# A transformer layer on one core: its first norm spread over ScalarE and GpSimd, and its first two tiles in written order

## The chip, the core and the metric

The kernel runs on one core of a Trainium2 chip. The core has five engines that are meant here: TensorE (PE, with its weight loads as PEld), VectorE (DVE), ScalarE (ACT), GpSimd (POOL), and SyncE (SP), which issues most DMAs. The metric is the device time of one execution in microseconds (us); a time given for a kernel is the median of several executions.

## What is computed

One layer of a diffusion transformer over 512 latent tokens (`x`) and 256 context tokens (`ctx`), model width 2048, all in float32. Cut to what matters here:

```python
sc_ = jax.nn.silu(c); scc = jax.nn.silu(c_ctx)
mod_x = (sc_ @ w_ada[l] + b_ada[l])[:, None, :]
mod_c = (scc @ w_ada[l] + b_ada[l])[None, None, :]
...
h  = _modulate(_rmsnorm(x, norm1_w[l]), sh1, s1)       # h * (1 + scale) + shift
hc = _modulate(_rmsnorm(xc, norm1_w[l]), sh1c, s1c)
q_da, k_da, v_da, q_mla, k_mla, v_mla = _mixer_inputs(h, tabs, *proj)
...
o_da = _sweep(lambda qb: _diff_attend(qb, k_da_all, v_da_all, lam), q_da)
o_mla = _sweep(lambda qb: _softmax_attend(qb, k_mla_all, v_mla_all, MLA_SCALE), q_mla)
x = x + g1 * (_merge_heads(o_da, o_mla, subln_w[l], lambda_init) @ w_o[l])
h2 = _modulate(_rmsnorm(x, norm2_w[l]), sh2, s2)
x = x + g2 * _conv_ffn(h2, w_up[l], conv_w[l], conv_b[l], w_down[l])
return _rmsnorm(x, final_w)
```

The normalised input needs a sum of squares over all 2048 features of each token, and a shift and a scale for each feature, which are products of `silu(c)` and `silu(c_ctx)` with columns of `w_ada`.

## The kernel before

Tokens lie along the free dimension. The 2048 features are 16 tiles (`kt`) of 128 partitions; `xs[kt]` (128x512) holds a tile of the latents, and `cs[kt // 2]` (128x512) the 256 context tokens of two tiles. A float32 product is made of three matmuls on parts (`mm3`, lines 101 to 106): each operand is split into a high part of type `F32R` (ScalarE) and the rest (VectorE, function `split`, lines 75 to 84).

**The beginning** (lines 266 to 314) stands inside `tc.manual_schedule`, so its engines take it in written order.
- SP loads the rows `c` and `c_ctx`, then all token tiles, then the first rows and columns of `w_ada`.
- ScalarE takes a Silu of both raw rows (line 282, one partition, 2048 long), TensorE spreads them over 128 partitions by a matmul with ones (line 287), and copies bring them to `cb` and `ccb` (lines 301 and 303).
- ScalarE squares each latent tile (line 293) and every second context half (line 295), VectorE squares the other halves (line 297) and adds 128x768 to one running sum `sqs` (line 299).
- TensorE sums `sqs` over the partitions by a matmul with ones (line 306). `rstd` (lines 157 to 164) makes 1/sqrt of it: Ln and Exp on ScalarE, one Newton step on VectorE. The result is `rinv`.

**Scales and shifts.** `scales(u)` makes the scale columns `a1` of two tiles by small TensorE products (`products`, line 206), a copy of `row` on ScalarE (line 208), two tiny matmuls (line 210) and a VectorE step (line 218). The shifts `modx` and `modc` of a tile come in one of two ways (`shifts`): for an even tile VectorE multiplies and reduces rows of `w_ada` (line 242, a half of 1024 at a time; one for the latents and one for the context), for an odd tile TensorE transposes the rows (line 258) and makes products. `modulation(u)` does both for two tiles and loads and splits the weights `w_g0` of these.

**The first weight products** (lines 344 to 367). For each tile VectorE makes `h` (line 358), ScalarE adds the shift and rounds to the high part (line 360), VectorE makes the low part (line 361), and TensorE adds the tile's contribution to five latent and four context accumulators (`mm3`, 27 matmuls). Outside `manual_schedule` a scheduler orders each engine's instructions.

**Later.** The other input projections follow, with the values last: their halves are split by ScalarE (`kh`) and VectorE (`kl`) and written to memory `v_d` (line 498), in the second half by GpSimd's queue. Then the first attention (`da_head`): the query, key and value parts of a head are read back (lines 543 to 558), with keys in `ks` and in the half-zero tile `klz` (cleared on GpSimd, line 534), scores are matmuls of line 510, the maximum is VectorE's (line 512), the exponential ScalarE's (line 514). `feature` makes the queries of the next head from `w_f` and calls `ahead(2)`, which issues the loads of the next weight blocks.

Of the kernel before, what the change touches and what calls it, by code (L numbers as in the profile page):

```python
# [17 lines left out]
P = 128  # L18
# [34 lines left out]
def layer_kernel(ctx: ExitStack, tc: tile.TileContext, small, rope, c_row, cc_row, x_t, ctx_t, ada, ada_k,  # L53
# [32 lines left out]

    def wblock(src, cols=1024, pool=None):
        pool, full = (pool, cols) if pool else (wp, 1024)
        raw = pool.tile([P, full], F32, tag="wr", name=nm("wr"), bufs=3 if full == 1024 else 2)
        nc.sync.dma_start(raw[:, :cols], src)  # L90
# [66 lines left out]
    def rstd(out, ssq, dim, t1, t2):  # L157

        sc.activation(out, ssq, AF.Ln, bias=epst, scale=1.0 / dim)
        sc.activation(out, out, AF.Exp, scale=-0.5)  # L160
        ve.tensor_scalar(out=t1, in0=ssq, scalar1=1.0 / dim, scalar2=EPS, op0=ALU.mult, op1=ALU.add)
# [50 lines left out]
    def scales(u, ws=None):  # L212

        ws = ws or columns(u)
# [6 lines left out]
    def columns(u):  # L221
        ws = []
        for j in range(4):
# [13 lines left out]
    def shift(kt, ws, i):  # L237

        d, vec = (modx, modc)[i][:, kt:kt + 1], (cb, ccb)[i]
        for hf, w in enumerate(ws):  # L240
            t = w if i else st.tile([P, D // 2], BF16, tag="junk", name=nm("junk"), bufs=1)
            ve.tensor_tensor_reduce(out=t, in0=w, in1=vec[:, hf * D // 2:(hf + 1) * D // 2], op0=ALU.mult,
                                    op1=ALU.add, scale=1.0, scalar=d if hf else col("b_ada", kt), accum_out=d)

    def shifts(kt):
# [4 lines left out]
        if kt % 2 == 0:  # L250
            for i in range(2):
                shift(kt, ws, i)
# [10 lines left out]

    with tc.manual_schedule(engines={mybir.EngineType.PE, mybir.EngineType.Activation, mybir.EngineType.DVE,
                                     mybir.EngineType.SP}):
# [9 lines left out]
        first_rows, first_columns = rows(0), columns(0)  # L277
# [3 lines left out]
        for wide in (cb, ccb):  # L281
            sc.activation(wide[0:1], wide[0:1], AF.Silu)
# [5 lines left out]
        exp_ln_tables()  # L288
        sqs = st.tile([P, TT], F32, tag="h", name="sqs", bufs=3)
        for kt in range(KT):  # L290
            sq = st.tile([P, TT], F32, tag="h", name=nm("sq"), bufs=3) if kt else sqs
            c = cs[kt // 2][:, (kt % 2) * C:(kt % 2 + 1) * C]
            sc.square(sq[:, :T], xs[kt])
            if kt % 2:
                sc.square(sq[:, T:], c)
            else:
                ve.tensor_tensor(sq[:, T:], c, c, op=ALU.mult)
            if kt:
                ve.tensor_tensor(sqs, sqs, sq, op=ALU.add)
            if kt in (8, 10, 12, 14):  # L300
                ve.tensor_copy(*spread.pop(0))
        while spread:
            sc.copy(*spread.pop(0))
        ssq = s_tile()
        for c0, c1 in ((0, T), (T, TT)):
            pe.matmul(ssq[:, c0:c1], ones32, sqs[:, c0:c1], start=True, stop=True)
        shift(0, first_rows, 0)
# [4 lines left out]
    g0b = [b_tile() for _ in range(4)]  # L312
    acc = g0b[3]
    g0w = []

    def modulation(u):
        if u:
            shifts(2 * u)
        scales(u, None if u else first_columns)
        g0w.append(wblock(w_g0[2 * u], 640, st))  # L320
        shifts(2 * u + 1)
        g0w.append(wblock(w_g0[2 * u + 1], 640, st))

    modulation(0)
    nc.sync.dma_start(silu_c, cb[0:1])
    nc.sync.dma_start(ropet, rope)
# [13 lines left out]
    hx, hc = [], []  # L340
    g0s = [s_tile(), s_tile()]
    lat0 = [g0s[0][:, :512], g0s[0][:, 512:], g0s[1][:, :512], g0s[1][:, 512:], g0b[0]]
    ctx0 = [g0b[1][:, :C], g0b[1][:, C:], g0b[2][:, :C], g0b[2][:, C:]]
    for kt in range(KT):
        if kt % 2 == 0 and kt < KT - 2:
            modulation(kt // 2 + 1)
        ct = cs[kt // 2][:, (kt % 2) * C:(kt % 2 + 1) * C]
        if kt % 2 == 0:
            chh, chl = c2k(F32R), c2k(F32R)
        o = (kt % 2) * C  # L350
        hx.append((a2k(F32R), a2k(F32R)))
        hc.append((chh[:, o:o + C], chl[:, o:o + C]))
        with tc.high_priority():
            h = st.tile([P, TT], F32, tag="h", name=nm("h"), bufs=3)
            for i, (x, c, m, (hh, hl)) in enumerate(((xs[kt], slice(0, T), modx, hx[kt]),
                                                     (ct, slice(T, TT), modc, hc[kt]))):
                b, t, r = m[:, kt:kt + 1], h[:, c], rinv[:, c]
                ve.scalar_tensor_tensor(out=t, in0=x, scalar=a1[:, 2 * kt + i:2 * kt + i + 1], in1=r,
                                        op0=ALU.mult, op1=ALU.mult)
                sc.activation(hh, t, AF.Identity, bias=b)  # L360
                ve.scalar_tensor_tensor(out=hl, in0=t, scalar=b, in1=hh.bitcast(F32), op0=ALU.add, op1=ALU.subtract)
        wh, wl = g0w[kt]
        for f in range(5):
            w = (wh[:, f * P:(f + 1) * P], wl[:, f * P:(f + 1) * P])
            mm3(lat0[f], w, hx[kt], kt == 0, kt == KT - 1)
            if f < 4:
                mm3(ctx0[f], w, hc[kt], kt == 0 and f % 2 == 0, kt == KT - 1, skip=True)
# [89 lines left out]
    def feature(lat, ctxo):  # L457
# [8 lines left out]
        ahead(2)  # L466
# [63 lines left out]

    klz = [da.tile([P, 2, TT], F32R, name=nm("klz")) for _ in range(2)]
    for t in klz:
        for i, r in enumerate((hi, lo)):
            gp.memset(t[r, i].bitcast(F32), 0.0)
# [4 lines left out]
    def da_queries(h):  # L539
        if h == 0:  # L540
            qs = [da.tile([P, T], F32R, tag=f"qs{i}", name=nm("qs"), bufs=2) for i in range(2)]
            for i in range(2):
                nc.sync.dma_start(qs[i].bitcast(F32), q0_d[i])
            return qs
        lat = b_tile("f", 2)
        feature(lat, None)
# [4 lines left out]
    def da_head(h, qs):  # L551
        ks = da.tile([P, 2, TT], F32R, tag="ks", name=nm("ks"), bufs=2)
        kl = klz[h % 2]
        for i, r in enumerate((lo, hi)):
            nc.sync.dma_start(ks[r].bitcast(F32), k_d[h][0].rearrange("(i p) n -> p i n", i=2))
            nc.sync.dma_start(kl[r, i].bitcast(F32), k_d[h][1][r])
# [857 lines left out]
```

## Time and profile before

| What | us |
|---|---|
| median of 3 executions | 2441.83 (2437.65 to 2445.8) |
| profiled execution, its own time | 2441.33 |
| its span in the profile | 2439.6 |
| TensorE busy | 2367.0 (97%) |
| VectorE busy | 1735.5 (71%) |
| ScalarE busy | 1117.0 (46%) |
| GpSimd busy | 220.2 (9%) |
| mean granted TensorE clock | 0.992 |

A timeline row gives the start in us from the span's start, the time it took, the engine, the line of the kernel, the operation, `out<-in` by tile names, the size, and how often it follows itself; in brackets the time for which the engine sat idle before it and what ended that. A float32 matmul of the row "x4" is two matmuls of two passes each. A row of waits reads: engine and line, what it waited for, us in total, times, longest. Matmuls overlap, so their steps are read from start to start.

### The profile page before, as it was taken

The numbers are of one execution on the slowest core, as the hardware profiler recorded it, in microseconds if no ns is written. First come the engines' busy times: TensorE is split into PE (matmuls) and PEld (weight loads), VectorE is DVE, ScalarE is ACT, GpSimd is POOL, SyncE is SP. The second block draws the span as 40 slices with busy tenths as digits, with TensorE's granted clock in tenths as the row PEclk, the third lists the DMA queues.
The fourth block names the chain that finished last, engine by engine and source line by source line (L and its number), as shares of the span: only waits on it lengthen the run. The fifth ranks groups of instructions, "written<-read, shape, count | busy, mean of one in ns | idle before, by whom it ended". The sixth has DMA issues, their size and how long they took to land.

```text
span 2439.6 us, 32889 instructions
## 1 busy us (share of the span) xinstructions
PE 2367.0 (97%) x12758; PEld 1978.4 (81%) x12758; DVE 1735.5 (71%) x2316; ACT 1117.0 (46%) x1696; POOL 220.2 (9%) x244
## 2 busy tenths in 40 slices
PE   6999999999999999999999999999999999999998
PEld 3678877777777778889888888888888888888888
DVE  6668876388868878378667676767666666666667
ACT  4432121155646542245445454545454545454545
POOL 0000000121100003100111111111111111111110
PEclk9999999999999999999999999999999999999999
DMA  8758889555411149423555555555555565556573
GB/s 300 279 211 309 327 319 330 181 166 144 127 59 44 44 161 349 146 87 113 147 130 143 134 140 137 137 139 136 141 134 143 132 143 132 141 135 140 133 188 111
DMA packets 130707, 403.32 MB, mean 165 GB/s; under 512 B 14323, under 2 KB 25075, under 8 KB 122099
## 3 DMA queue, kind: packets, MB, share of 16 engines
q1 hardware_dynamic: 104118, 350.87, 43.7%
q0 software_dynamic: 25280, 49.30, 11.6%
q8 instruction: 100, 1.64, 0.3%
q10 hardware_dynamic: 1152, 1.05, 0.1%
q14 instruction: 57, 0.47, 0.1%
HBM read 331.68 MB, written 69.48 MB: 164 GB/s over the span
## 4 chain that ended last, share of the span: by engine, by line
PE 76%; DVE 8%; issue 7%; ACT 4%; DMA 3%; POOL 2%; SPq 0%; DVEq 0%; ACTq 0%; POOLq 0%
PE y L1133 11%; PE b L105 9%; PE b L104 9%; PE b L106 9%; PE z L1133 5%; PE y L1135 5%; PE s L104 3%; PE s L105 3%; PE s L106 3%; PE z L1135 3%; PE s L510 3%; PE x L1133 2%; DMA ada<-in_ada 2%; PE b L206 1%; PE f L104 1%
## 5 line engine op out<-in xcount | busy, mean ns | idle before, releaser
L989 DVE TENSOR_TENSOR wl<-wr,wh 128x1024 fp32r<-128x1024 f32 x144 | 176.4, 1225 | 157.8 <-ACT wh L981 157.1
L981 ACT CAST wh<-wr 128x1024 fp32r<-128x1024 f32 x144 | 151.0, 1049 | 234.0 <-PE b L105 118.5
L104 PE MATMUL b<-ah,wh 128*128 128x512 f32 (+1 forms) x664 | 256.8, 387 | 0.0
L105 PE MATMUL b<-al,wh 128*128 128x512 f32 (+1 forms) x664 | 256.7, 387 | 0.0
L106 PE MATMUL b<-ah,wl 128*128 128x512 f32 (+1 forms) x664 | 255.9, 385 | 0.0
L1154 POOL DMA_DIRECT2D x_d<-xs x160 | 139.6, 1004 | 1162.6 <-ACT xs L1153 1159.3
L989 DVE TENSOR_TENSOR wl<-rb,wh 128x1024 fp32r<-128x1024 f32 x123 | 150.0, 1220 | 126.9 <-ACT wh L981 126.8
L981 ACT CAST wh<-rb 128x1024 fp32r<-128x1024 f32 x123 | 129.2, 1050 | 185.7 <-PE b L105 116.1
L989 DVE TENSOR_TENSOR wl<-ws,wh 128x1024 fp32r<-128x1024 f32 x123 | 150.1, 1220 | 90.1 <-ACT wh L981 90.1
L80 ACT CAST wh<-wr 128x1024 fp32r<-128x1024 f32 (+3 forms) x102 | 99.2, 972 | 217.0 <-PE b L106 62.1
L171 DVE CUSTOM_DVE_ANT_0 ada<-ada,cb,smt 128x2048 f32<-128x2048 f32 x64 | 152.5, 2382 | 54.6 <-DMA ada<-in_ada 54.2
L981 ACT CAST wh<-ws 128x1024 fp32r<-128x1024 f32 x123 | 128.2, 1043 | 130.3 <-DVE ws L943 44.3
L1133 PE MATMUL y<-a2k,wh 128*128 128x512 f32 x656 | 164.0, 392 | 0.0
L81 DVE TENSOR_TENSOR wl<-wr,wh 128x1024 fp32r<-128x1024 f32 (+3 forms) x102 | 116.9, 1146 | 62.1 <-ACT wh L80 61.7
L104 PE MATMUL b<-a2k,wh 128*128 128x512 f32 (+1 forms) x376 | 141.6, 377 | 5.9 <-ACT a2k L838 4.3
L106 PEld LDWEIGHTS b<-ah,wl 128*128 128x128 f32 x664 | 124.8, 188 | 25.7
L104 PEld LDWEIGHTS b<-ah,wh 128*128 128x128 f32 x664 | 125.1, 188 | 22.9
L105 PEld LDWEIGHTS b<-al,wh 128*128 128x128 f32 x664 | 125.1, 188 | 21.9
L105 PE MATMUL b<-a2k,wh 128*128 128x512 f32 (+1 forms) x376 | 140.8, 374 | 0.0
L106 PE MATMUL b<-a2k,wl 128*128 128x512 f32 (+1 forms) x376 | 140.0, 372 | 0.0
L1133 PEld LDWEIGHTS y<-a2k,wh 128*128 128x128 f32 x656 | 118.6, 189 | 21.6
L1133 PE MATMUL y<-b2k,wh 128*128 128x512 f32 x410 | 107.8, 393 | 0.0
(454 smaller groups left out, 5757.2 us busy)
## 6 DMA issues: line engine op xcount, KB each, us to landing
ada<-in_ada SPq DMA_DIRECT2D x64, 1024.0 KB, 6.4
rb<-in_w_up SPq DMA_DIRECT2D x123, 512.0 KB, 4.3
wr<-in_w_dn SPq DMA_DIRECT2D x88, 512.0 KB, 4.3
x_d<-xs POOLq DMA_DIRECT2D x160, 256.0 KB, 6.0
wr<-in_w_up SPq DMA_DIRECT2D x53, 512.0 KB, 4.2
wr<-in_w_f SPq DMA_DIRECT2D x34, 512.0 KB, 6.0
ada<-in_ada SPq DMA_DIRECT2D x32, 512.0 KB, 6.4
adak<-in_ada_k SPq DMA_DIRECT2D x32, 512.0 KB, 6.3
```

The lines of the kernel that those rows point to most:

```text
L80: sc.copy(dst_h, src)
L81: ve.tensor_tensor(dst_l, src, dst_h.bitcast(F32), op=ALU.subtract)
L104: pe.matmul(out, st[0], mv[0], start=start, stop=False, **kw)
L105: pe.matmul(out, st[0], mv[1], start=False, stop=False, **kw)
L106: pe.matmul(out, st[1], mv[0], start=False, stop=stop, **kw)
L171: ve.tensor_tensor_reduce(out=junk, in0=w, in1=vec, op0=ALU.mult, op1=ALU.add, scale=1.0, scalar=col("b_ada", j), accum_out=dst[:, j:j + 1])
L510: pe.matmul(s[:, c0:c1], a, b[:, c0:c1], start=i == 0, stop=i == len(mms) - 1)
L981: sc.copy(t, raw[:, k * n_:k * n_ + n_])
L989: ve.tensor_tensor(t, raw[:, k * n_:k * n_ + n_], hi[k].bitcast(F32), op=ALU.subtract)
L1133: pe.matmul(o, w[j][0], hs[j], start=start and j == 0, stop=False, skip_group_check=True)
L1135: pe.matmul(o[:, h0], w[j][1], hs[j][:, h0], start=False, stop=j == 7, skip_group_check=True)
L1154: gp.dma_start(x1_d[dt], x, accum_op=ALU.add)
```

## The change

- **Raw rows.** TensorE spreads the raw `c` and `c_ctx`, and ScalarE takes the Silu of the spread rows as it moves them out of PSUM (128x512 each, eight of them), between its squares.
- **Squares.** Each latent square goes to a tile of its own, so ScalarE does not wait for VectorE. GpSimd squares the context tiles (128x512, two tiles at once). VectorE keeps two running sums, one of the latents and one of the context; the last two latent squares are not added by VectorE but go to TensorE's column sums, which become five matmuls.
- **`rstd`** takes a piece of work to put between its VectorE steps: the first half of tile 0's shift.
- **Written order.** The first two tiles, with shifts of both by VectorE, `scales(0)`, `scales(1)` and the first products, now stand inside `manual_schedule`, which holds GpSimd too. Their loads are issued in written order. In tiles 0 and 1 the five latent products stand ahead of the four context ones. `modulation(1)` keeps shifts and weights of tiles 2 and 3 alone; `silu_c` and `ropet` are moved behind it.
- **First attention.** Tiles of the pool `da` are laid out in another order, `klz` is cleared by VectorE, and the loads of the weight blocks behind head 1's queries are issued after the key loads of head 0.

```diff
-    def rstd(out, ssq, dim, t1, t2):
+    def rstd(out, ssq, dim, t1, t2, beside=None):
...
         ve.tensor_scalar(out=t1, in0=ssq, scalar1=1.0 / dim, scalar2=EPS, op0=ALU.mult, op1=ALU.add)
+        if beside:
+            beside()
         ve.scalar_tensor_tensor(out=t2, in0=out, scalar=-0.5, in1=out, op0=ALU.mult, op1=ALU.mult)
...
-            sc.activation(wide[0:1], wide[0:1], AF.Silu)
...
-        for kt in range(KT):
-            sq = st.tile([P, TT], F32, tag="h", name=nm("sq"), bufs=3) if kt else sqs
-            c = cs[kt // 2][:, (kt % 2) * C:(kt % 2 + 1) * C]
-            sc.square(sq[:, :T], xs[kt])
-            if kt % 2:
-                sc.square(sq[:, T:], c)
+        for p in range(KT // 2):
+            qc = c2k()
+            gp.tensor_tensor(qc, cs[p], cs[p], op=ALU.mult)
+            if p >= 6:
+                sc.activation(*spread[p], AF.Silu)
+            qs = [square(2 * p), square(2 * p + 1)]
+            if p < 6:
+                sc.activation(*spread[p], AF.Silu)
+            if p == 0:
+                sx, sc_ = qs[0], qc
             else:
-                ve.tensor_tensor(sq[:, T:], c, c, op=ALU.mult)
-            if kt:
-                ve.tensor_tensor(sqs, sqs, sq, op=ALU.add)
+                ve.tensor_tensor(sc_, sc_, qc, op=ALU.add)
+            for q in qs[p == 0:]:
+                if p == KT // 2 - 1:
+                    sums.append(q)
+                else:
+                    ve.tensor_tensor(sx, sx, q, op=ALU.add)
...
+        for i, q in enumerate([sx] + sums):
+            pe.matmul(ssq[:, :T], ones32, q, start=i == 0, stop=i == 2)
+            if i == 1:
+                for j in range(2):
+                    pe.matmul(ssq[:, T:], ones32, sc_[:, j * C:j * C + C], start=j == 0, stop=j == 1)
...
-        rstd(rinv, ssq[:, :TT], D, nt1, nt2)
-        shift(0, first_rows, 1)
+        rstd(rinv, ssq, D, nt1, nt2, lambda: shift(0, first_rows[0], 0, 0))
+        shift(0, first_rows[0], 0, 1)
...
+        for kt in range(2):
+            homes(kt)
+            if kt:
+                for hf in range(2):
+                    shift(1, first_rows[1], 0, hf)
+                g0w.append(split_block(raw1, 640, st))
+            scaled(kt, 0)
+            scaled(kt, 1)
+            shifted(kt, 0)
+            for hf in range(2):
+                shift(kt, first_rows[kt], 1, hf)
+            shifted(kt, 1)
+            if kt:
+                scales(1, second_columns)
+            g0_products(kt)
...
-        ahead(2)
+        with tc.issue_after(behind) if behind else nullcontext():
+            ahead(2)
...
-            gp.memset(t[r, i].bitcast(F32), 0.0)
+            ve.memset(t[r, i].bitcast(F32), 0.0)
+    key_loads = []
```

Here `scaled(kt, i)` is the `h` step of the latents (`i` = 0) or the context (1), `shifted(kt, i)` the high and low parts, `shift(kt, ws, i, hf)` one half of a VectorE reduction, and `g0_products(kt)` the 27 matmuls of a tile.

How it moves instructions, at three places. First VectorE at the start, before:

```order
L297 TENSOR_TENSOR sqs<-c2k_162 128x256
L299 TENSOR_TENSOR sqs<-sqs,sq_241 128x768
L297 TENSOR_TENSOR sq_245<-c2k_168 128x256
L299 TENSOR_TENSOR sqs<-sqs,sq_245 128x768
L299 TENSOR_TENSOR sqs<-sqs,sq_249 128x768
```

and of the change, the same place (`a2k_254` is the latents' running sum, `c2k_252` the context's):

```order
L364 TENSOR_TENSOR a2k_254<-a2k_254,a2k_256 128x512
L359 TENSOR_TENSOR c2k_252<-c2k_252,c2k_260 128x512
L364 TENSOR_TENSOR a2k_254<-a2k_254,a2k_262 128x512
L364 TENSOR_TENSOR a2k_254<-a2k_254,a2k_264 128x512
L359 TENSOR_TENSOR c2k_252<-c2k_252,c2k_270 128x512
L364 TENSOR_TENSOR a2k_254<-a2k_254,a2k_272 128x512
```

VectorE no longer squares; it adds narrower tiles, and each context sum waits for a square by GpSimd. Second ScalarE around tiles 0 and 1. Before (`a2k_524` and `c2k_522` are tile 0's latent and context high parts, `a2k_560` tile 1's, `row_458` belongs to `scales(1)`):

```order
L360 ACTIVATE a2k_524<-h_526,modx 128x512
L259 COPY wt_364<-b_331 128x512
L335 ACTIVATE ls<-ls 128x2
L259 COPY wt_364<-b_331 128x512
L360 ACTIVATE c2k_522<-h_526,modc 128x256
L208 COPY row_401<-b_331 128x128
L360 ACTIVATE a2k_560<-h_562,modx 128x512
L360 ACTIVATE c2k_522<-h_562,modc 128x256
L208 COPY row_458<-b_331 128x256
```

and of the change (`a2k_382` and `c2k_380` with `h_384` are tile 0, `h_422` tile 1, `row_455` belongs to `scales(1)`):

```order
L284 ACTIVATE a2k_382<-h_384,modx 128x512
L284 ACTIVATE c2k_380<-h_384,modc 128x256
L80 CAST wh_427<-wr_227 128x640
L80 CAST wh_509<-wr_507 128x640
L284 ACTIVATE a2k_420<-h_422,modx 128x512
L80 CAST wh_561<-wr_559 128x640
L284 ACTIVATE c2k_380<-h_422,modc 128x256
L217 COPY row_455<-b_351 128x256
```

On TensorE the tiny matmuls that read `row_458` stood behind the products of tile 1; those that read `row_455` now stand ahead of tile 1's first product. Third SP ahead of the first head of attention, before:

```order
L90 DMA wr_3757<-in_w_f 128x1024
L90 DMA wr_4043<-in_w_f 128x1024
L90 DMA wr_4049<-in_w_f 128x1024
L90 DMA wr_4291<-in_w_f 128x1024
L90 DMA wr_4297<-in_w_f 128x1024
L543 DMA qs_3815<-q_d 128x512
L543 DMA qs_3816<-q_d 128x512
L555 DMA ks_3819<-k_d_128 64x2x768
```

and of the change (`wr_3728` is the block that was `wr_3757`, `wr_4016` the one that was `wr_4043`):

```order
L89 DMA wr_3728<-in_w_f 128x1024
L614 DMA qs_3782<-q_d 128x512
L614 DMA qs_3783<-q_d 128x512
L627 DMA ks_3784<-k_d_128 64x2x768
L628 DMA klz_3785<-k_d_128 64x768
L627 DMA ks_3784<-k_d_128 64x2x768
L628 DMA klz_3785<-k_d_128 64x768
L630 DMA v_3797<-v_d_136 128x1536
L89 DMA wr_4016<-in_w_f 128x1024
```

The head's own loads now leave ahead of four weight blocks.

More of the change, by code (lines that the diff above doesn't have):

```diff
@@ L210, in products, with scales @@
             pe.matmul(acc[:, 2 * i:2 * i + 2], row[:, i * P:(i + 1) * P], sel, start=True, stop=True)
[L212 to L214 removed]
+    def scales(u, ws):
         products(lambda kt: ws[kt // 4][:, kt % 4], 2 * P)
@@ L302, in layer_kernel, with square @@
[L302 to L307, printed above, removed]
+        def square(kt):
+            q = a2k()
+            sc.square(q, xs[kt])
+            return q
+        sums = []
+        for p in range(KT // 2):
[8 more added lines that the diff above has]
+                sx, sc_ = qs[0], qc
+            else:
+                ve.tensor_tensor(sc_, sc_, qc, op=ALU.add)
[4 more added lines that the diff above has]
+                    ve.tensor_tensor(sx, sx, q, op=ALU.add)
@@ L329, in layer_kernel @@
+    def modulation(u):
+        if u > 1:
+            scales(u, columns(u))
+        for kt in (2 * u, 2 * u + 1):
+            shifts(kt)
+            g0w.append(wblock(w_g0[kt], 640, st))
     lt = cst.tile([P, 64], F32, name="lt")
@@ L338, in layer_kernel @@
     ve.tensor_scalar(out=subs, in0=col("sub"), scalar1=1.0 - LAMBDA_INIT, scalar2=None, op0=ALU.mult)
[L340 to L344, printed above, removed]
+    modulation(1)
+    for kt in range(2, KT):
         if kt % 2 == 0 and kt < KT - 2:
             modulation(kt // 2 + 1)
[L347 to L352, printed above, removed]
-        with tc.high_priority():
[L354 to L367, printed above, removed]
+        if kt == 6:
+            nc.sync.dma_start(silu_c, cb[0:1])
+            nc.sync.dma_start(ropet, rope)
+        homes(kt)
+        with tc.high_priority():
+            for i in range(2):
+                scaled(kt, i)
+                shifted(kt, i)
+        g0_products(kt)
     st.release()
```

111 lines of the change are left out of this document (74 added, 37 removed).

## The prediction

> **What bounds the kernel now.** I read the busy time by stretch first, then what TensorE waited for, then the timeline of the two places that the edit touches. In the rows by stretch the columns are the stretch, its length, and the busy time of TensorE, its weight loads, VectorE, ScalarE and GpSimd, then the granted clock, the DMA share and GB/s.
>
> ```profile
> PE 2367.0 (97%) x12758; PEld 1978.4 (81%) x12758; DVE 1735.5 (71%) x2316; ACT 1117.0 (46%) x1696; POOL 220.2 (9%) x244
> ```
>
> ```profile
> 0.00:45.00 45.00, 23.69 (x68) 10.28 (x68) 30.18 (x54) 25.51 (x41) 1.15 (x7) 0.95 0.76 283
> ...
> 100.00:200.00 100.00, 97.92 (x749) 72.53 (x748) 70.15 (x128) 43.12 (x76) 0.00 (x0) 1.00 0.65 231
> ```
>
> ```profile
> PE s L306 <- DVE sqs L299: 10.4, 1, 10.4
> ...
> PE s L510 <- DMA ks<-k_d: 4.6, 1, 4.6
> ```
>
> TensorE is busy for 97% of the span, so the edit can win only where TensorE stands or runs at half clock: ahead of the first weight products (23.69 us busy of 45, nearly all of it small helpers), and at the first attention scores (L510). Between these two it is full, and whatever the start gains or loses is carried to the end unchanged.
>
> ```profile
> 6.65 0.43 DVE L297 TENSOR_TENSOR sqs<-c2k 128x256 f32<-128x256 f32 x1 [1.93 <-DMA c2k<-in_ctx_t]
> ...
> 15.76 0.33 SPq L273 DMA_DIRECT2D a2k<-in_x_t  x1
> ...
> 30.50 0.95 DVE L299 TENSOR_TENSOR sqs<-sqs,sq 128x768 f32<-128x768 f32 x1
> ...
> 31.50 2.93 PE L306 MATMUL s<-sqs,ones 128*128 128x512 f32 x4 [10.38 <-DVE sqs L299]
> ...
> 34.47 0.90 ACT L159 ACTIVATE rinv<-s,epst 128x768 f32<-128x768 f32 x1 [2.99 <-PE s L306]
> ...
> 45.33 1.22 PE L104 MATMUL s<-a2k,wh 128*128 128x512 f32 x2
> ...
> 65.69 0.73 PE L104 MATMUL s<-a2k,wh 128*128 128x512 f32 x2 [0.76 <-ACT a2k L360]
> ```
>
> ```profile
> a2k<-in_x_t SPq DMA_DIRECT2D x16, 256.0 KB, 5.2
> ```
>
> The start is a chain: VectorE's sum of squares ends at 31.5, though the last token tile has landed by 15.76 + 5.2 = 21.0; column sums on TensorE to 34.4; Ln to 35.4; first products at 45.3. The last row is the first matmul of tile 2 (the third of 16). It is my common mark: before it, tiles 0 and 1 and the scales of tiles 2 and 3 are done in either kernel, and behind it the same work follows.
>
> **Part 1, up to the Ln.** The edit takes two 1x2048 Silus off ScalarE's path, and squares the context on GpSimd. VectorE keeps 19 sums of 128x512 up to the total that TensorE needs first. ScalarE's 16 squares and eight spreads stay ahead of landing and cost nothing: they are issued as the tiles land, and VectorE, behind them, ends later. TensorE's spreads start when the raw rows land instead of after a Silu, and nothing on this chain waits for them. The loads that change places on SP (first `w_g0` ahead of the last two column blocks, `silu_c` and `ropet` later) land by 30 as now, well ahead of their readers. The question is what VectorE and GpSimd do to each other. Before has no such squares; the nearest rows are GpSimd's two-input sums near 920 us.
>
> ```profile
> 496.55 0.67 DVE L151 TENSOR_TENSOR rt<-rt,ropet 128x512 f32<-128x512 f32 x1
> ...
> 918.38 2.35 DVE L171 CUSTOM_DVE_ANT_0 ada<-ada,cb,smt 128x2048 f32<-128x2048 f32 x1
> 919.27 2.62 POOL L705 TENSOR_TENSOR ss<-ss,sq 128x512 f32<-128x512 f32 x1
> ...
> 923.11 3.38 DVE L171 CUSTOM_DVE_ANT_0 ada<-ada,cb,smt 128x2048 f32<-128x2048 f32 x1
> ...
> 924.87 2.77 POOL L705 TENSOR_TENSOR ss<-ss,sq 128x512 f32<-128x512 f32 x1
> ...
> 1005.66 1.29 POOL L705 TENSOR_TENSOR ss<-ss,sq 128x512 f32<-128x512 f32 x1
> ```
>
> Alone a GpSimd op takes 1.29. The one at 919.27 begins inside a VectorE op with two SBUF inputs that ends at 920.7, and ends at 921.9, 1.2 later: it stood until the other was through. The VectorE op at 923.11 stretches from 2.35 to 3.38 the same way. So I take the two as excluding each other, and their times add: 19 x 0.67 = 12.7 and 8 x 1.29 = 10.3, together 23.0 from the first landed context tile at 6.65, that is 29.6. About 1 us of idle at the start and 1 us of overlap between neighbouring VectorE ops cancel. The bounds: 21.5 if they don't touch (landing sets it), and 41 if every square held the pair for the 2.77 of the row at 924.87. I take **29.6**, 1.9 earlier than now.
>
> The Trainium skill, "Advanced Engine Details and Errata", section GPSIMD Details, says that GpSimd shares a read and a write interface with VectorE and conflicts with VectorE ops that have two SBUF inputs. It speaks against this change, the rows above agree with it, and without it the sum would be that of the first rival.
>
> The column sums grow: three of 512 and two of 256 columns, 2048 where 768 took 2.93.
>
> ```profile
> 184.77 1.50 PE s L435 x4
> ```
>
> ```profile
> 48.00:50.00 2.00, 2.00 (x33) 1.39 (x32) 1.22 (x3) 0.43 (x2) 0.00 (x0) 0.50 0.92 328
> 50.00:52.00 2.00, 2.00 (x14) 1.60 (x11) 0.57 (x4) 0.71 (x2) 0.00 (x0) 0.90 1.02 349
> ```
>
> ```profile
> 494.00:496.00 2.00, 2.00 (x11) 0.96 1.09 270
> ```
>
> That is 7.8 at the speed of L306, or 4.0 at that of L435 (768 columns in 1.50, the clock full). After a pause TensorE runs at half clock for some 5 us: from 45.3 to about 50.4, and from 488.95 to 494 (the last row: stretch, length, TensorE, clock, DMA). So 5.1 us do 65% of it and the rest takes 1.4: 6.5. Ln then ends at 29.6 + 6.5 + 0.95 = **37.0**, against 35.4 now: 1.6 later.
>
> **Part 2, from the Ln to tile 2.** Now the order is as written, and VectorE carries it. Tile 1's shifts come from VectorE reductions in place of TensorE transposes; this frees some 3 us of TensorE work that now lies beside other waits, so I count nothing for it. What counts is what was put in a row: `scales(1)` stands behind both shifts of tile 1, and on ScalarE its `row` copy stands behind tile 1's context activation, which needs `modc`, the last of VectorE's reductions. TensorE has all of tile 1 queued behind that copy.
>
> ```profile
> 35.40 0.96 DVE L161 TENSOR_SCALAR nt<-s 128x768 f32<-128x768 f32 x1 [1.42 <-ACT rinv L159]
> ...
> 53.38 1.28 DVE L242 CUSTOM_DVE_ANT_0 junk<-ada,cb,smt 128x1024 bf16<-128x1024 f32 x1
> ...
> 54.70 1.28 DVE L242 CUSTOM_DVE_ANT_0 junk<-ada,cb,modx 128x1024 bf16<-128x1024 f32 x1
> ...
> 62.62 0.37 ACT L208 COPY row<-b 128x256 f32<-128x256 f32 x1 [9.94 <-PE b L206]
> ...
> 63.04 0.61 PE L210 MATMUL b<-sel,row 128*128 128x2 f32 x4 [0.55 <-ACT row L208]
> ...
> 64.14 1.40 DVE L358 SCALAR_TENSOR_TENSOR h<-a2k,a,rinv 128x512 f32<-128x512 f32 x2
> ...
> 65.86 0.74 DVE L361 SCALAR_TENSOR_TENSOR a2k<-h,modx,a2k 128x512 fp32r<-128x512 f32 x1
> ...
> 66.01 0.51 ACT L360 ACTIVATE c2k<-h,modc 128x256 fp32r<-128x256 f32 x1
> ...
> 67.32 0.82 DVE L81 TENSOR_TENSOR wl<-wr,wh 128x640 fp32r<-128x640 f32 x1
> ```
>
> ```profile
> 53.77 0.28 PE L106 MATMUL b<-c2k,wl 128*128 128x256 f32 x1
> ...
> 53.89 0.40 PE L104 MATMUL b<-a2k,wh 128*128 128x512 f32 x1
> ...
> 54.12 0.39 PE L105 MATMUL b<-a2k,wh 128*128 128x512 f32 x1
> ```
>
> On VectorE between the Ln and that `modc`: ten half reductions at 1.27 from start to start (four of tile 0, four of tile 1, and two of tile 2 that the scheduler puts between) are 12.7; four passes of the norm 3.9; two weight splits 1.5; four `h` 2.2; two low halves of latents 1.4; the `a` columns and one context low half 0.9 by their size; two waits for ScalarE's high half 1.1. That is 23.7. ScalarE's context activation 0.5, `row` 0.4 and the two tiny products 0.6 follow: tile 1 starts on TensorE 25.2 after the Ln. Tile 0 and the products of `scales(1)` are done by 19 after the Ln, so TensorE stands some 5 us and comes back at half clock. Tile 1 is 15 matmuls 0.23 apart and 12 at 0.115, 4.8; the 5.1 us at half clock cost another 2.5. Tile 2 begins at 37.0 + 25.2 + 7.3 = **69.5**, against 65.7: **+3.8 us**. If the clock stays up it is +1.3; if TensorE's waits fell apart further (one more reduction between), +5.
>
> **Part 3, the first scores.** Not in the title, but in the diff.
>
> ```profile
> 476.95 0.95 SPq L543 DMA_DIRECT2D qs<-q_d  x2
> ...
> 487.33 0.69 DVE L81 TENSOR_TENSOR kl<-b,kh 128x512 fp32r<-128x512 f32 x1 [2.50 <-DMA v_d<-kl]
> ...
> 488.95 0.76 PE L510 MATMUL s<-ks,qs 128*128 128x512 f32 x1 [4.60 <-DMA ks<-k_d]
> ...
> 489.10 3.09 POOL L534 MEMSET klz<- 64x768 f32 x4
> ...
> 492.14 0.90 ACT L514 ACTIVATE p<-s,m 128x768 f32<-128x768 f32 x1 [4.45 <-DVE m L512]
> ```
>
> On SP four weight loads go behind the head's query, key and value loads, which then leave after the second of six loads, some 30 us earlier, and their tiles lie where no late reader holds them. The 4.6 us wait goes, and with it 5.1 us at half clock (2.6): 7.2, and the value writes lose a rival for the DMA engines. What is late next: the zeroing of `klz`, now on VectorE behind the last `kl` split (487.33 here, which itself waited for a write). Its price on VectorE is not in the trace; I bound it by nothing and by GpSimd's 0.77 a piece (a quarter of 3.09). With the writes quicker I expect a wait of 0 to 2 and take 0.3. And the next head's weights, loaded later, no longer fill the gaps of the softmax: after the two first scores TensorE waits for the first exponential (0.6, behind a maximum and 0.9), for the second (0.4), for the combined weights that it transposes (1.9) and for the low part of a late weight block (1.0): about 3.9 us in the first 10, worked out by laying the new order out with these durations. So 7.2 - 3.9 - 0.3 = **-3.0 us**; bounds 0 (the splits end as late as now) and -5 (the gaps get filled).
>
> **Sum.** 2441.33 (profiled execution: span 2439.6 and 1.7 around it) + 3.8 - 3.0 = 2442.1; that execution lies 0.5 below the median of 2441.83. I predict **2442**.
>
> **Rivals.**
> 1. *VectorE and GpSimd pass each other.* Then the sum of squares ends at 21.5, the Ln at 28.9, and tile 2 starts at 61.4: -4.3, with part 3 -7.3: 2434. For it: squares and sums read different tiles. Against it: four overlapped ops near 920 that all stretched. Chance 0.15, and half of it would cross 0.3%.
> 2. *The exclusion is dearer.* If each square costs the pair 2.77 instead of 1.29, the sum ends at 41 and the whole start moves by 11.4: 2453. It crosses 0.3% from 2.1 us a square (sum at 36.2, so 6.6 later and 2448.7). Against it: 2.77 holds the other engine's time already. Chance 0.12.
> 3. *Part 3 does not do what it says:* the write chain of the values ends as late as now, and TensorE waits for the zeroing where it waited for keys. Then 2445. For it: the second head's loads still fall between these writes. Chance 0.2.
>
> **How the numbers follow.** My case has 0.53. A measurement of this kernel tells about 0.3%, 7.3 us, from no change (the three runs span 8.2). My case and rival 3 lie inside it; rival 1 half, rival 2 mostly outside, and for order effects that I can't see in the 110 us behind tile 2 I give each side 0.08: faster 0.17, same 0.65, slower 0.18. The range 2432 to 2450 takes in rival 1, rival 3 and the first half of rival 2.
>
> **What would show it.** Right: GpSimd's squares stretched beyond 1.29 and the sum ending near 29 to 30; the column sums over 6 to 7 us; `row` of `scales(1)` right behind the context activation, TensorE idle before it, granted clock 0.5 after it; tile 2 near 69; the key wait at the first scores gone. Wrong: the sum at 22, a TensorE that never pauses between tiles 0 and 1, or a wait for `klz` of 4 us and more.

## The result, and the profile after

The changed kernel takes **2446.44 us** (median of 15 executions, 2440.61 to 2450.56), the kernel before 2439.13 (15, 2436.43 to 2445.8). The ratio of the two is 1.0026 with a 95% interval of 1.0017 to 1.0035: **6.3 us slower**, 4.1 to 8.5. The forecast was 2442, and its sum +0.8: the time lies inside the range, but the sum is 5.5 us short. The profiled execution of the change has a span of 2447.7, 8.1 longer than that of before.

The same instruction in both timelines (its start in us from the span's start) tells where the 8.1 came from:

| Instruction | before | changed | difference |
|---|---|---|---|
| TensorE takes the sum of squares | 31.50 | 26.91 | -4.6 |
| Ln | 34.47 | 33.34 | -1.1 |
| first product of tile 0 | 45.33 | 43.07 | -2.3 |
| first product of tile 2, the prediction's mark | 65.69 | 66.33 | +0.6 |
| first column sum of the latent norm, behind tile 15 | 180.57 | 176.75 | -3.8 |
| last column sum of the query latents' norm | 339.68 | 341.71 | +2.0 |
| first product of the attention's first `feature` | 473.99 | 481.68 | +7.7 |
| first score | 488.95 | 494.20 | +5.3 |

The rest of the 8.1 lies behind the first score, where TensorE now waits for the softmax (3.6 us between 493 and 520). These marks of the start differ by some 2.5 us from profile to profile: four kernels with this changed beginning (three of them are among the experiments) have tile 2 at 63.85 (`bank_free`), 65.22 (`start_alone`), 65.78 (`gemv_later`) and 66.33 (the change).

The start, in the timeline of the changed kernel:

```profile
7.11 1.04 POOL L350 TENSOR_TENSOR c2k<-c2k 128x512 f32<-128x512 f32 x1 [5.38 <-DMA c2k<-in_ctx_t]
...
8.44 0.69 DVE L364 TENSOR_TENSOR a2k<-a2k,a2k 128x512 f32<-128x512 f32 x1 [3.67 <-ACT a2k L344]
...
10.20 0.69 DVE L359 TENSOR_TENSOR c2k<-c2k,c2k 128x512 f32<-128x512 f32 x1 [1.07 <-POOL c2k L350]
...
13.03 1.40 POOL L350 TENSOR_TENSOR c2k<-c2k 128x512 f32<-128x512 f32 x1 [0.64 <-DMA c2k<-in_ctx_t]
13.46 3.06 DVE L364 TENSOR_TENSOR a2k<-a2k,a2k 128x512 f32<-128x512 f32 x2
...
26.91 3.78 PE L368 MATMUL s<-a2k,ones 128*128 128x512 f32 x4 [9.07 <-DVE a2k L364]
...
32.19 1.11 PE L368 MATMUL s<-a2k,ones 128*128 128x512 f32 x2
...
33.34 0.90 ACT L166 ACTIVATE rinv<-s,epst 128x768 f32<-128x768 f32 x1 [10.03 <-PE s L368]
...
43.07 0.80 PE L111 MATMUL s<-a2k,wh 128*128 128x512 f32 x1 [6.41 <-ACT a2k L284]
...
56.93 0.72 ACT L80 CAST wh<-wr 128x640 fp32r<-128x640 f32 x1 [4.83 <-DMA wr<-in_w_g]
57.56 0.50 ACT L284 ACTIVATE c2k<-h,modc 128x256 fp32r<-128x256 f32 x1
57.97 0.35 ACT L217 COPY row<-b 128x256 f32<-128x256 f32 x1
58.38 1.01 PE L219 MATMUL b<-sel,row 128*128 128x2 f32 x4 [5.17 <-ACT row L217]
59.25 0.77 PE L111 MATMUL s<-a2k,wh 128*128 128x512 f32 x1
...
66.33 0.48 PE L111 MATMUL s<-a2k,wh 128*128 128x512 f32 x1
```

Squares and sums stretch each other. The row copy stands behind tile 1's context activation, and TensorE stands 5.17 for it; some 0.4 of this is a weight split (56.93), whose block landed late and which stands ahead of that activation. Between the last row and the latent norm nothing was expected, and here the scale products of a pair of tiles stand in one run, where before had four pieces between larger matmuls. In both fences the last row is the first column sum of the latent norm. The kernel before:

```profile
73.41 0.39 PE L106 MATMUL b<-a2k,wl 128*128 128x512 f32 x1
73.73 0.64 PE L206 MATMUL b<-adak,cpad 128*32 128x256 f32 x8
74.30 0.49 PE L104 MATMUL s<-a2k,wh 128*128 128x512 f32 x1
...
180.57 1.56 PE L435 MATMUL s<-nq,ones 128*128 128x512 f32 x4 [0.51 <-ACT nq L433]
```

The changed kernel:

```profile
73.92 0.28 PE L112 MATMUL b<-c2k,wh 128*128 128x256 f32 x1
74.13 1.93 PE L215 MATMUL b<-adak,cpad 128*32 128x256 f32 x32
75.99 0.39 PE L113 MATMUL b<-c2k,wl 128*128 128x256 f32 x1
...
176.75 1.56 PE L498 MATMUL s<-nq,ones 128*128 128x512 f32 x4 [0.56 <-ACT nq L496]
```

From the matmul ahead to the one behind, a piece of 8 takes 74.30 - 73.41 = 0.89, of which the large matmul's own step is 0.23: 0.66, so 2.6 for four pieces. The run of 32 takes 75.99 - 73.92 - 0.12 = 1.95. Over six pairs of tiles that is some 4.1 us, about the 4.5 by which the difference fell from +0.6 to -3.8. From tile 2 to the latent norm before takes 114.9 and the change 110.4; the other three profiles of this beginning take 112.1 to 112.4, so there the gain is 2.5 to 2.8.

Two new waits come later. First the query latents' norm in the changed kernel:

```profile
336.02 1.04 ACT L80 CAST wh<-wr 128x1024 fp32r<-128x1024 f32 x1 [7.73 <-DMA wr<-in_w_v]
336.97 0.58 ACT L543 COPY cq<-b 128x512 f32<-128x512 f32 x1
337.45 0.63 ACT L496 ACTIVATE nq<-cq 128x512 f32<-128x512 f32 x1
...
338.13 2.07 PE L498 MATMUL s<-nq,ones 128*128 128x512 f32 x2 [4.17 <-ACT nq L496]
```

On ScalarE the split of a weight block that landed late stands ahead of the third latent's copy and square, for which TensorE waits 4.17; its column sums then take 2.07 (1.12 before), at half clock. Not all of the difference is kept: between 400 and 420 the kernel before also stands, and runs at half clock for a part of the stretch. The stretch (length, TensorE's busy time, granted clock, DMA share, GB/s) in before:

```profile
400.00:420.00 20.00, 17.90 (x71) 0.91 1.01 309
```

and in the changed kernel:

```profile
400.00:420.00 20.00, 18.91 (x84) 1.00 0.95 299
```

Second comes the attention's first product, in the timeline of the changed kernel:

```profile
480.94 0.69 DVE L81 TENSOR_TENSOR kl<-b,kh 128x512 fp32r<-128x512 f32 x1 [1.01 <-DMA v_d<-kl]
481.68 0.80 PE L111 MATMUL f<-a2k,wh 128*128 128x512 f32 x1 [8.07 <-DVE kl L81]
...
494.20 0.39 PE L574 MATMUL s<-ks,qs 128*128 128x512 f32 x1
```

TensorE stood 8.07 us until VectorE had made the last `kl`, the low part of the values, and then ran at half clock for some 4.5 us. The key wait ahead of the first score is gone, as forecast. The stretches around it in the changed kernel, with the same columns:

```profile
470.00:480.00 10.00, 3.61 (x16) 0.81 0.49 197
480.00:490.00 10.00, 8.32 (x27) 0.68 0.71 250
```

### The profile page after: what moved, and what is told of

It is laid out like the page before. It is cut to its first block, busy times and chain, and to the rows that moved or that the text cites. A ratio compares the mean times of both kernels' runs of the same rounds, so it can differ in the third digit from the quotient of the medians.

```text
span 2447.7 us, 32794 instructions
## 1 busy us (share of the span) xinstructions
PE 2362.7 (97%) x12714; PEld 1982.6 (81%) x12714; DVE 1739.4 (71%) x2319; ACT 1111.4 (45%) x1685; POOL 231.5 (9%) x248
## 3 DMA queue, kind: packets, MB, share of 16 engines
q0 software_dynamic: 25280, 49.30, 11.5%
## 4 chain that ended last, share of the span: by engine, by line
PE 79%; DVE 9%; DMA 5%; ACT 3%; issue 2%; POOL 1%; SPq 0%; DVEq 0%; ACTq 0%; POOLq 0%
PE y L1205 12%; PE b L111 9%; PE b L112 9%; PE b L113 9%; PE z L1205 6%; PE y L1207 6%; PE z L1207 3%; DMA ada<-in_ada 3%; PE s L111 3%; PE s L112 3%; PE s L113 3%; PE s L574 3%; PE x L1205 2%; DVE m L576 1%; POOL p L639 1%
## 5 line engine op out<-in xcount | busy, mean ns | idle before, releaser
L111 PEld LDWEIGHTS b<-ah,wh 128*128 128x128 f32 x664 | 125.1, 188 | 22.9
```

The source lines that it names most:

```text
L111: pe.matmul(out, st[0], mv[0], start=start, stop=False, **kw)
```

## Experiments

Ratios are to executions of the kernel before on the same chip.

| Kernel | us | ratio | interval |
|---|---|---|---|
| `bank_free` | 2434.67 | 0.9980 | 0.9968 to 0.9993 |
| `bank_taken_before` | 2448.52 | 1.0035 | 1.0023 to 1.0047 |
| `scores_alone` | 2438.54 | 0.9987 | 0.9977 to 0.9997 |
| `start_alone` | 2436.34 | 0.9986 | 0.9974 to 0.9998 |
| `scales_first` | 2435.50 | 0.9978 | 0.9968 to 0.9988 |
| `row_early` | 2435.23 | 0.9973 | 0.9961 to 0.9985 |
| `gemv_later` | 2436.92 | 0.9976 | 0.9965 to 0.9986 |
| `scales_scores` | 2434.56 | 0.9973 | 0.9962 to 0.9984 |
| `mixed` | 2428.70 | 0.9944 | 0.9930 to 0.9959 |
| `mixed_sums_first` | 2429.15 | 0.9949 | 0.9935 to 0.9963 |

**The wait ahead of the first feature product.** Its PSUM tile `f` lies in bank 6 in both programs. As the tile addresses of the built programs show (a profile doesn't print them), the pool gives its banks out in the order in which tiles are first written. Of tile 0's three accumulators in this pool, before writes a context one first, the change the fifth latent one. From there the rotation of the banks differs, and the last two value accumulators lie in 4 and 7 before, in 4 and 6 after. `bank_free` moves the fifth latent product of tiles 0 and 1 back behind the context ones, and the banks are those of before:

```diff
-        for f, i in sorted(jobs, key=lambda j: j[1]) if kt < 2 else jobs:
+        for f, i in sorted(jobs, key=lambda j: (j[0] == 4, j[1])) if kt < 2 else jobs:
```

> The changed kernel; only tile 0's order differs: the fifth latent product stands behind the four context ones, so PSUM banks are taken in the order of before. My theory: the 8.1 us for which TensorE stood ahead of the first feature product came from its PSUM bank, which the last value splits still read. Then that wait is gone, the feature products start by 475, no half clock stands behind it, and the time is 2433 to 2437. Rival: the moved loads and the zeroing hold the value splits up, and whichever comes first waits for them; then the wait turns up at the first scores (8 us in all) and the time stays at 2445 to 2447.

Measured 2434.67, and the waits of TensorE no longer have the row. The timeline of `bank_free`:

```profile
465.96 0.39 PE L111 MATMUL f<-a2k,wh 128*128 128x512 f32 x1
...
473.44 0.69 DVE L81 TENSOR_TENSOR kl<-b,kh 128x512 fp32r<-128x512 f32 x1 [1.01 <-DMA v_d<-kl]
```

The feature products run while the last splits, up to 474, are still to come. Of the ratios, 1.0026 / 0.9980 = 1.0046: the bank cost **11.2 us** (by the two intervals 3.8 on either side). The wait of 8.07 and half of the 4.5 us at half clock behind it make 10.3. The counter-test gives the kernel before the bad bank:

```diff
-        for f in range(5):
+        for f in range(5) if kt else (4, 0, 1, 2, 3):
```

> The kernel before; only tile 0's order of feature blocks differs (the fifth first), which puts the last value accumulators and the first feature product of the attention into one PSUM bank. My theory: the feature product must now wait from 474 to the last value split at 488, the key wait of 4.6 us goes, and half clock follows: 2447 to 2454. Rival (the bank is not the cause): 2438 to 2441, with the key wait of 4.6 us still there.

Measured 1.0035, 8.5 us slower (5.6 to 11.5), with this row among TensorE's waits, and no key wait:

```profile
PE f L104 <- DVE kl L81: 13.9, 1, 13.9
```

Both directions agree, so the rival is out.

**The two parts apart.** `scores_alone` is before with the diff's last part (and the layout of the pool `da`); `start_alone` is `bank_free` with that part taken out. The lines that stand in the one and are missing in the other, beside the order in which `o`, `rt`, `qs` and `ks` are laid out:

```diff
-        ahead(2)
+        with tc.issue_after(behind) if behind else nullcontext():
+            ahead(2)
...
-            gp.memset(t[r, i].bitcast(F32), 0.0)
+            ve.memset(t[r, i].bitcast(F32), 0.0)
```

> The kernel before with the third part of the change alone (tiles laid out ahead, zeroing on VectorE, four weight loads behind the key loads); its beginning and its PSUM banks are those of before. The prediction's third part: 3.0 us faster (bounds 0 and 5), 2434 to 2439. Rival: the value writes end as late as now and TensorE waits for the zeroing, or the late weights cost what the keys gave: 2439 to 2443.

> The changed beginning alone, with PSUM banks as before and the first attention as before. My theory: the first projection ends some 4 us earlier, and this lead is given back at the norm of the third latent (TensorE waits 4 us for a square that stands on ScalarE behind a late weight block, and half clock follows), so 2437 to 2440. The prediction's first part (3.8 us slower): 2441 to 2444. If the lead survived: 2434 to 2436.

`scores_alone` is 3.2 us faster (0.7 to 5.6), as forecast. Its first scores do not wait for keys or for the zeroing, and the waits behind them came as predicted: 3.6 us up to 500, where 3.9 were forecast. TensorE's waits between 478 and 660, in before:

```profile
PE s L510 <- DMA ks<-k_d: 4.6, 1, 4.6
PE pt L522 <- DVE p L568: 4.4, 6, 2.1
```

and in `scores_alone`:

```profile
PE pt L523 <- DVE p L576: 6.9, 9, 2.1
PE s L511 <- ACT p L515: 1.3, 1, 1.3
```

In the one profile the gain is smaller: its first score comes 5.1 earlier than in before, and its span is 1.8 shorter (2437.8 against 2439.6).

`start_alone` is 3.4 us faster (0.5 to 6.3) where the prediction had 3.8 slower; 2436.34 lies between a lead that survives and one that is given back. In its profile TensorE waits 1.5 for the third latent's square, against 4.2 in the changed kernel and none in `bank_free`. The work there is the same in all three, so that wait differs from one execution to the next, and I do not charge it to the median.

**Where the start's gain comes from.** `scales_first` is before with one line moved, to where the change has it:

```diff
     def modulation(u):
+        scales(u, None if u else first_columns)
         if u:
             shifts(2 * u)
-        scales(u, None if u else first_columns)
```

> The kernel before; only in modulation the scale products are written ahead of the even tile's shift, as in the change. On TensorE the 32 small products of a pair of tiles then stand in one or two runs instead of four pieces of 8 between larger matmuls. My theory: each piece costs some 0.17 us more than in one run, so the first projection (the first column sum of the latent norm, at 180.6 in before) ends some 4 us earlier, at 176 to 177.5. Rival: the pieces cost nothing and the 4.5 us that the change gained behind tile 2 come from elsewhere; then 180 to 181.

It is 5.4 us faster (2.9 to 7.8). Its timeline has most of the products in one run, and the latent norm 5.6 earlier than before:

```profile
73.05 1.93 PE L206 MATMUL b<-adak,cpad 128*32 128x256 f32 x32
...
175.00 1.56 PE L435 MATMUL s<-nq,ones 128*128 128x512 f32 x4 [0.51 <-ACT nq L433]
```

The norm is earlier than the 176 to 177.5 that I expected: the pieces explain some 4 of the 5.6, and the rest is not traced.

`scales_scores` adds the last part of the diff to it: of the changed beginning it has nothing but this order.

> The kernel before with scales_first and the third part of the change; no raw rows spread early, no squares on GpSimd, no written order of tiles 0 and 1. If what the beginning of the change gained came from the run of small products alone, and the written beginning itself costs about 2 us (first column sum of the latent norm at 175.0 here, against a mean of 177.2 in the kernels with the written beginning): 2431 to 2434, some 2 us below bank_free. If the written beginning gains something of its own: 2435 to 2437.

At 0.9973 it can't be told from `bank_free` (0.9980) by time, and 2434.56 lies between my two forecasts. By the profile its latent norm stands at 174.4, against 175.9, 176.8, 177.2, 177.6 and 178.2 in the five kernels with the written beginning of the change (`bank_free`, the change, `row_early`, `start_alone`, `gemv_later`): the beginning by itself seems to cost some 2.5 us there. That rests on single profiles, which differ by 2.3 among these five, and the times do not show it.

**What squares and sums do to each other.**

```diff
-            gp.tensor_tensor(qc, cs[p], cs[p], op=ALU.mult)
+            for _ in range(2):
+                gp.tensor_tensor(qc, cs[p], cs[p], op=ALU.mult)
```

> The changed kernel with each GpSimd square of the context issued twice into the same tile, so 8 more GpSimd ops in the same stretch. The prediction's exclusion (times add): the sum of squares, which TensorE takes at 26.9 in the change, ends at 35 or later. My reading now (an add and a square that overlap cost VectorE some 0.5 us a square): at 29 to 32. No interplay: 26.5 to 28.

One execution, 2452.84. The timeline of `squares_twice`:

```profile
19.76 8.71 POOL L351 TENSOR_TENSOR c2k<-c2k 128x512 f32<-128x512 f32 x6
...
21.71 2.97 DVE L365 TENSOR_TENSOR a2k<-a2k,a2k 128x512 f32<-128x512 f32 x2
...
33.07 3.78 PE L369 MATMUL s<-a2k,ones 128*128 128x512 f32 x4 [15.30 <-DVE a2k L365]
```

Where GpSimd squares without a pause, a square takes 8.71 / 6 = 1.45 (1.04 alone) and an add 2.97 / 2 = 1.48 (0.69 alone). If they excluded each other for the whole of both, a pair would take 1.04 + 0.69 = 1.73. The sum ends 6.2 later than in the change, 0.77 for each of the eight added squares, between the first two expectations: less than exclusion, more than I read from the change. Whether the two run at the same time or take turns for a part of each, no run here shows.

**The wait for `row`.** `row_early` is `bank_free` with tile 1's scales first:

```diff
             if kt:
+                scales(1, second_columns)
                 for hf in range(2):
                     shift(1, first_rows[1], 0, hf)
...
-            if kt:
-                scales(1, second_columns)
             g0_products(kt)
```

> bank_free with the scales of tiles 2 and 3 written ahead of tile 1's shifts. The prediction's second part (TensorE stands 5 us for the row copy behind tile 1's context activation, then half clock): the 5.2 us wait for row goes, tile 1's latent products start at 53, and its context products wait for the context activation at 58 instead; first product of tile 2 by 61 to 64 (66.3 in the change), first projection done 2 to 4 us earlier, 2431 to 2434. Rival (VectorE's chain of reductions sets tile 2 anyway): tile 2 within 1 us of 66.3 and the time within 1 us of bank_free, 2434 to 2436.

By the time the rival holds: 0.9973, the latent norm at 177.15. By tile 2 neither does: it starts at 72.33, 6.0 later than in the change, since TensorE now takes transposes of a later tile ahead of tile 1's products and among them, and waits for their rows to land. VectorE, in written order, now waits for the product that TensorE waited for, and everything behind it moves back. Timeline of `row_early`:

```profile
53.06 0.47 DVE L226 TENSOR_SCALAR a<-b,b,smt 128x2 f32<-128x2 f32 x2 [6.47 <-PE b L219]
...
58.26 0.80 PE L111 MATMUL s<-a2k,wh 128*128 128x512 f32 x1 [2.68 <-ACT a2k L284]
...
72.33 0.40 PE L111 MATMUL s<-a2k,wh 128*128 128x512 f32 x1
```

**The memory stream.** `gemv_later` is `bank_free` with three 1 MB loads moved from the query latents to the values' second half:

```diff
-        next_gemv(kv, 2)
+        next_gemv(kv, 1)
...
-            next_gemv(kv, 1 if (half * 8 + kb) % 3 else 2)
+            next_gemv(kv, 2 if half or kb % 3 == 0 else 1)
```

> bank_free with three of the 1 MB rows of later reductions moved from the three query latents to the second half of the values. My theory: the wait at the norm of the third latent (4.2 us in the change's profile, and not there in every execution) comes from a memory stream that is full from 200 to 340 us; with less in it the wait never occurs, the time falls to 2431 to 2434 and the executions lie closer together. Rival (nothing is late there in bank_free): no difference, 2434 to 2436.

No gain (0.9976), and the executions lie no closer together (2427.92 to 2439.11; `bank_free` 2430.73 to 2442.74). Since `bank_free`'s own profile has no wait at that norm, this does not test my theory of it; why the weight block landed late in one execution stays open.

**A version that beats both.** `mixed` is the change with part 1 kept, and tiles 0 and 1 taken out of the written order: `scales(0)`, shifts, splits and products go back to `modulation(0)` and the scheduler, with their loads; scales stand ahead of shifts, and the banks are as in before.

```diff
-        for kt in range(2):
-            homes(kt)
...
-            g0_products(kt)
...
-    modulation(1)
-    for kt in range(2, KT):
+    modulation(0)
...
+    for kt in range(KT):
```

> As scales_scores, but with the first part of the change too (raw rows spread by TensorE, Silus on the way out, squares on GpSimd, five column sums); tiles 0 and 1 are left to the scheduler, with the scales ahead of the shifts. My theory: the sums up to the Ln are 1 to 2 us faster than in before, and it was the written order of tiles 0 and 1 that cost, so the Ln starts by 33.5, the latent norm's first sum stands at 173 to 174.5, and the time is 2429 to 2433. Rival: the first part gains nothing that reaches the end of the first projection; then 175 and 2431 to 2434.

It takes 2428.70, 13.7 us less than before (10.0 to 17.1), and 6 less than `scales_scores`. But the reason that I gave fails: its Ln starts later than in before. Timeline of `mixed`:

```profile
25.07 2.23 PE L215 MATMUL b<-adak,cpad 128*32 128x256 f32 x16 [7.18 <-DMA adak<-in_ada_k]
...
35.53 0.90 ACT L166 ACTIVATE rinv<-s,epst 128x768 f32<-128x768 f32 x1 [4.68 <-PE s L363]
...
169.21 1.56 PE L478 MATMUL s<-nq,ones 128*128 128x512 f32 x4 [0.51 <-ACT nq L476]
```

TensorE waits 7.18 for columns ahead of the column sums, and yet the latent norm comes at 169.2, 5.2 before `scales_scores`. TensorE's busy time by stretch, `mixed`:

```profile
0.00:45.00 45.00, 29.34 (x110) 0.95 0.93 355
45.00:70.00 25.00, 24.88 (x198) 0.88 0.73 254
```

and `scales_scores`:

```profile
0.00:45.00 45.00, 23.73 (x67) 0.96 0.88 324
45.00:70.00 25.00, 21.86 (x158) 0.94 0.74 253
```

The first product comes at the same time in both (45.70 and 45.68). Ahead of it TensorE is busy for 5.6 us more, of which some 2.7 are the wider column sums (5.6 against 2.9); behind it 3.0 more is done in 25 us: `scales_scores` waits there, 2.2 of it for tile 2's high part, and `mixed` has next to no gap. `mixed_sums_first` puts the first scale products behind the column sums:

```diff
         rstd(rinv, ssq, D, nt1, nt2, lambda: shift(0, first_rows[0], 0, 0))
+        scales(0, first_columns)
         shift(0, first_rows[0], 0, 1)
...
-        scales(u, columns(u) if u else first_columns)
+        if u:
+            scales(u, columns(u))
```

> As mixed, with the first scale products (which TensorE waited 7.2 us for in mixed, their columns landing late) written behind the column sums, in front of tile 0. If the sum of squares bounds this start: the Ln starts near 32.7 instead of 35.5, the latent norm's first sum near 167 instead of 169.2, and the time is 2425 to 2428. If what counts is that TensorE's small work for tiles 0 and 1 is done while it must wait anyway (mixed had 29.3 us of TensorE work in the first 45, scales_scores 23.7): the first projection ends as late as in mixed or later, 169 to 173, and the time is 2428 to 2433.

The timeline of `mixed_sums_first`:

```profile
33.42 0.88 ACT L166 ACTIVATE rinv<-s,epst 128x768 f32<-128x768 f32 x1
...
168.57 1.56 PE L480 MATMUL s<-nq,ones 128*128 128x512 f32 x4 [0.51 <-ACT nq L478]
```

and its TensorE by stretch:

```profile
0.00:45.00 45.00, 26.82 (x76) 0.94 0.90 339
45.00:70.00 25.00, 25.00 (x240) 0.97 0.89 310
```

Its Ln is 2.1 earlier than in `mixed`, its latent norm 0.6, its time the same. So an earlier sum is worth little here, and so is small work done ahead of tile 0, of which it has no more than `scales_scores` once the wider column sums (6.6 from 26.68 on) are taken off. What both mixed kernels share is a TensorE without a gap between 45 and 70, and the scale products of tiles 2 and 3 in one run (at 52.25 and 49.80), where `scales_scores` has four pieces up to 58.11. That this order closes the gap is a guess: no run takes the parts from each other.

## Why the prediction was right on the range and wrong in its terms

- **Sum of squares, 29.6 forecast, 26.9 measured.** Inside the bounds 21.5 and 41, but GpSimd cost VectorE 5.7 instead of 10.3: 1.1 of waiting for the second square, and 4.6 by which the last six stretched VectorE's adds (18 adds from 10.20 to 26.77, where adds beside an idle GpSimd stand 0.66 apart). Of the 4.6 too much, 2.0 is the price: a square alone takes 1.04, and I had taken the 1.29 of a sum of two tiles. The rest is the step that failed, "I take the two as excluding each other, and their times add": a pair takes 1.45 to 1.48, and `squares_twice` pays 0.77 for a square of 1.04. On the other side the first add starts at 8.44 and not at 6.65, since it needs ScalarE's second square: 1.8, where the prediction had allowed 1 and set it off. The trace agrees in direction with the rule that the prediction cites from the Trainium skill, "Advanced Engine Details and Errata", section GPSIMD Details; here its price is less than the sum of both times.
- **Column sums, 6.5 forecast, 6.4 measured** (26.91 to the Ln at 33.34). Right, and by the mechanism: 1536 of the 2048 columns take 5.3 us, the last 512 take 1.1. The granted clock of 26 to 34 reads 1.00 all the same, so the half speed shows in the steps alone.
- **From the Ln to tile 1 on TensorE, 25.2 after its end forecast, 25.0 measured** (34.24 to 59.25), with a wait of 5.2 for `row` (5 forecast), and 7.1 more to tile 2 (7.3 forecast). Right: VectorE's chain to `modc` took 22.9 of the 23.7 forecast, and the late weight split gave 0.4 back. Of the 3.2 by which tile 2 comes earlier than forecast, 2.7 are the sum's.
- **"Behind it the same work follows": wrong, and the sign of the first term with it.** The same matmuls followed, but in another order, and this gained 4.5 between tile 2 and the latent norm (2.5 to 2.8 in the other profiles of this beginning). `scales_first` shows 5.4 (2.9 to 7.8) for that order alone. Of the three places at which the prediction looked at the order none lies there. So the start is -3.4 (`start_alone`) instead of +3.8: the scales' order pays more than the written beginning costs, which single profiles put at some 2.5.
- **First scores, -3.0 forecast, -3.2 measured** (`scores_alone`). The key wait is gone, the softmax waits are there (3.6, 3.9 forecast), the zeroing costs no wait. That the two totals agree so closely is partly luck, with an interval of 0.7 to 5.6.
- **The step that is missing: +11.2.** In part 3 I asked what is late next and named the zeroing; the first feature product, a piece ahead of it on TensorE, was late, since its bank had changed hands. Its cause is a line of the diff that I gave no price, the five latent products ahead of the context ones; the prediction took the loads and the zeroing for all that part 3 could change at this place. Rival 3 (2445) had the right time for the wrong reason: the write chain as the change has it does no harm in `bank_free`.
- **Sum by ratios:** -3.4 - 3.2 + 11.2 = +4.6, against +6.3 measured with 2.2 on either side. That 2446 lies inside 2432 to 2450 is luck: the start was 7.2 better than forecast, and the bank, which the prediction does not have, cost more than that. And the measurement told 6.3 us from no change, where the prediction had said that it takes 7.3.

Not settled: the wait at the query latents' norm, what `scales_first` gains beyond the pieces, whether the written beginning costs anything by itself, and the parts of `mixed`'s gain.

## What to carry to other kernels

An edit at the start of a kernel can be paid for 400 us later, by a buffer that a rotation gives to someone else: compare which PSUM bank each accumulator has before and after, wherever a tile of a new pool meets the last readers of the old one. When a mark divides a sum, check that what follows the mark also stands in the same order, not only that it is the same work. And here small products were cheaper in a run than in pieces between larger matmuls, so the line on which they are written is worth a test.

## What the hardware showed

A VectorE add of two SBUF tiles and a GpSimd square, each 128x512, take 0.69 and 1.04 alone, and 1.48 and 1.45 where GpSimd squares without a pause. Eight 128x256 products with 32 columns of weights, put between larger matmuls, cost 0.66; 32 in a run cost 1.95. In the change TensorE stood until 481.68, and its granted clock was 0.50 from 478 to 486 and 0.91 from 486 to 488; in `bank_taken_before` it stood until 486.13, and the clock was 0.50 from 480 to 492 and 0.99 from 492 to 494. So half clock began inside the wait and outlasted it by some 4.5 and 6 us.
